# Spreading eight attention heads 3, 3, 2, 0 instead of 2, 2, 2, 2 over the four pairs of convolution chunks

## The chip, the cores and the metric

The kernel runs on one core of a Trainium2 chip. The metric is the device time of one execution in microseconds (us). Engines are named as in the profile: PE multiplies matrices (PEld loads its weights), DVE, ACT and POOL do elementwise work, SP issues nearly all DMAs. Each engine works through its own instructions strictly in the order in which they stand.

## The reference

One decoder layer for 512 tokens of width 2048, all in float32. Cut to what matters here:

```python
mod = silu(c) @ w_ada + b_ada                       # 6 sections of 2048 columns
shift1, scale1, gate1, shift2, scale2, gate2 = split(mod, 6)
h = rms_norm(x, norm1_g) * (1 + scale1) + shift1
cb, cc, ch, aq, ak, av = split(h @ w_in, ...)       # six blocks of 1024 columns
y_conv = cb * causal_conv3(cc * ch, conv_w)         # 1024 columns: 8 chunks of 128
for head in range(8):                               # two softmaxes per head
    p1, p2 = softmax(mask(q1 @ k1.T)), softmax(mask(q2 @ k2.T))   # 512 x 512 each
    y_attn[head] = rms_norm((p1 - lam * p2) @ v) * subln_g * (1 - lam_init)
x = x + gate1 * (concat(y_conv, y_attn) @ w_out)
h2 = rms_norm(x, norm2_g) * (1 + scale2) + shift2
# product-key expert layer: top-16 keys for 8 heads, 16384 single-neuron experts
x = x + gate2 * peer_ffn(h2, w_peer_q, sub_keys1, sub_keys2, expert_u, expert_v)
```

## The kernel before

Matrix products with weights are done in three passes: a number is split into a high part (by ACT, line 89) and the rest (by POOL or DVE, line 90), and PE adds high*high, high*rest and rest*high (`PASSES`). So every weight tile that lands (`wraw`, up to four in flight) passes ACT and then POOL before PE has all of it (`wsp`, three of them), and so does every activation tile.

The stages in the order of the code: norm and the first part of the modulation; the projections for q, k and v; then, around line 530, the stage that is changed; then the output projection (lines 545 to 607); then the expert layer, which takes most of the time.

**The changed stage** is a loop over four pairs of convolution chunks, `cp` = 0 to 3:

```python
nxt_head = 0
for cp in range(4):
    for _ in range(HEADS[cp]):
        head(nxt_head)
        nxt_head += 1
    if cp == 3:
        gw_ctx.close()
        ...
        xy = xy_ctx.enter_context(tc.tile_pool(name="xy", bufs=2, side="right"))
    conv(cp)
    if cp < 3:
        ada_later(ADA_N.pop(0))
```

- `head(h)` (lines 452 to 493) does one attention head in four blocks of 128 queries. In each block PE makes scores for both softmaxes (`sp`, line 461, and a mask, 463), DVE takes the maximum (464), ACT the exponential (466), DVE combines the two (469 to 471, `qk`), PE transposes (475), ACT copies (477, `aT`), PE multiplies with `vv` (480), ACT copies (482, `osb`) and sums squares. At the end of the head ACT takes a root (485), DVE scales (486, 489), PE transposes (490), ACT copies (492, `yt`), and a DMA stores the head (493, `y_dram`).
- `conv(cp)` (496 to 528) multiplies 256 columns of each of three blocks of `w_in` with the activations (507, 288 matrix products of 128x512 for a pair) and does the short convolution on DVE (518 to 527); two DMAs store `y_dram`. It also issues DMAs that lay expert rows out anew in DRAM (`lay_out`, line 249).
- `ada(...)` (192 to 222), called by `ada_later`, makes 512 columns of the modulation that is needed later: eight loads of 512 KB (`ada_w`, line 200, three buffers), sixteen multiply-adds on DVE (211, 215, `ada_acc`), four tiny PE products (219) and an addition (221). Three of these follow each of the first three pairs, nine in all. `ada_acc` and `ada_w` live in the pool `gw`.
- The output projection starts with loads of the sixteen chunks of `y` (552, `yr`, in the order `WO_ORDER`: chunks 0 to 5, 8 to 15, then 6 and 7) and of `x` (577, `xr`, four loads), both into the pool `xy`, which takes the place of `gw`: they can be issued only when the last `ada` is done with its memory. `yr` is split (`big`). There are four groups (`dg`) of 192 matrix products (593); group 0 needs all sixteen chunks, the others use them again. Each group ends with four additions on DVE (599). Between them twelve tiles of expert rows are loaded (561, `uar`, eight DMAs of 128 KB each, three buffers), transposed on DVE (570) and stored (571, 1 MB). PE also transposes `x` (581).

A scheduler orders the instructions when the program is built, by an estimate of its own of when each can run, with the order of the code as priority. So a head, which mostly waits for its own chain of engines, is not done before `conv` but woven into it and into what follows, on every engine.

Of the kernel before, what the change touches and what calls it, by code (L numbers as in the profile page):

```python
# [40 lines left out]
LAG = 3  # L41
PASSES = ((0, 0), (0, 1), (1, 0))
ADA_LATER = (0, 0, 0, 1, 2, 2, 2, 3, 3, 3)
HEADS = (2, 2, 2, 2)
WO_ORDER = (0, 1, 2, 3, 4, 5, 8, 9, 10, 11, 12, 13, 14, 15, 6, 7)
UR_BUFS = 2
BEGIN = 1
# [32 lines left out]
def hymba_peer(tc, x, c, positions, w_ada, b_ada, norm1_g, w_in, conv_w, q_norm_g, k_norm_g,  # L80
# [18 lines left out]
    with ExitStack() as ctx:  # L99
# [431 lines left out]
# [3 lines that stand above are left out]
# [580 lines left out]
```

## Time and profile before

| what | value |
|---|---|
| three runs of before: median (lowest, highest) | 3346.73 us (3344.19, 3349.19) |
| profiled execution, its own time | 3349.88 us |
| its span in the profile | 3347.6 us |
| PE busy | 3176.0 us, 95% of the span |
| DVE, ACT, POOL busy | 2739.1, 1223.3, 1057.7 us |
| moved by DMA | 1017.81 MB, 304 GB/s over the span |
| mean granted PE clock | 0.978 |

The time of an execution and its span differ by 2.3 us, which lie around the program. A busy share of the whole span is a mean over stages that have different limits, so the changed stage is read in windows of its own: it goes from about 384 us (first scores) to 733 us (last convolution product), and the output projection follows to 947 us.

### The profile page before, as it was taken

Reading aid. Unit: us, or ns where it says so; the run is one execution under the profiler, and the core shown is the slowest. Engines: PE = TensorE matmul, PEld = TensorE weight load, DVE = VectorE, ACT = ScalarE, POOL = GpSimd, SP = SyncE. Lnnn points to the kernel's source line nnn. Section 1 sums busy time; section 2 is a strip of 40 time slices with the busy share of each in tenths; the row PEclk is TensorE's granted clock in tenths of the full one; section 3 lists DMA queues with packets and bytes.
Section 4 is the critical chain, followed back from the end, with each engine's and each line's share of the span. In section 5 each row is a group of like instructions: output and inputs, shape, how many; then the busy total and the mean of one; then the engine's idle time right before and its main releaser. Section 6 shows DMA issues by size and latency. Waiting matters only on the chain.

```text
span 3347.6 us, 47029 instructions
## 1 busy us (share of the span) xinstructions
PE 3176.0 (95%) x18006; PEld 2945.2 (88%) x18006; DVE 2739.1 (82%) x3631; ACT 1223.3 (37%) x1866; POOL 1057.7 (32%) x709
## 2 busy tenths in 40 slices
PE   5889999999999859999999999999999999999998
PEld 4777877777777659999999999999999999999997
DVE  6888477842338998789999899999999999999975
ACT  5246343343255336632333333333333333333322
POOL 2447333353435634312222232222222222222210
PEclk9999999999999979999999999999999999999998
DMA  9878978966979878989989899998988898999964
GB/s 303 283 257 294 345 250 280 299 211 221 315 256 302 261 243 288 335 290 364 343 332 343 310 333 363 325 338 323 340 333 316 336 354 329 360 330 338 338 222 158
DMA packets 388896, 1017.81 MB, mean 304 GB/s; under 512 B 29713, under 2 KB 108478, under 8 KB 328126
## 3 DMA queue, kind: packets, MB, share of 16 engines
q1 hardware_dynamic: 342590, 679.23, 59.8%
q0 software_dynamic: 46080, 335.56, 25.7%
q8 instruction: 141, 2.31, 0.3%
q14 instruction: 85, 0.70, 0.1%
HBM read 965.11 MB, written 171.18 MB: 339 GB/s over the span
## 4 chain that ended last, share of the span: by engine, by line
PE 55%; DVE 4%; issue 2%; DMA 1%; ACT 0%; POOL 0%; DVEq 0%; ACTq 0%; SPq 0%; POOLq 0%
PE pa L835 26%; PE pv L1004 26%; PE pv L974 2%; DVE gacc L910 1%; DVE ut L90 1%; DMA xs<-x_dram 1%; DVE gt L963 1%; DVE ur L823 1%; DVE vs L90 1%; DMA gt<-in_expert_v_dram,idxu 0%; DMA gt<-in_expert_u_dram,idxu 0%; ACT ut L89 0%; DVE acc L1020 0%; PE pv L1061 0%; DVE gt L897 0%
## 5 line engine op out<-in xcount | busy, mean ns | idle before, releaser
L835 PE MATMUL pa<-hd,ut 128*128 128x352 f32 x6144 | 1067.2, 326 | 37.5 <-DVE ut L90 23.6
L1004 PE MATMUL pv<-W,vs 128*128 128x352 f32 x6144 | 1052.1, 325 | 5.1 <-ACT W L89 2.6
L835 PEld LDWEIGHTS pa<-hd,ut 128*128 128x128 f32 x6144 | 1010.9, 190 | 42.4 <-DVE ut L90 26.6
L1004 PEld LDWEIGHTS pv<-W,vs 128*128 128x128 f32 x6144 | 1001.8, 189 | 8.0 <-ACT W L89 3.5
L90 POOL TENSOR_TENSOR wsp<-wraw,wsp 128x1024 fp32r<-128x1024 f32 x160 | 389.0, 2434 | 557.6 <-ACT wsp L89 525.4
L89 ACT ACTIVATE vs<-vr 128x1024 fp32r<-128x1024 f32 x256 | 271.6, 1061 | 737.9 <-PE pv L1004 687.8
L89 ACT ACTIVATE ut<-ur 128x1024 fp32r<-128x1024 f32 x256 | 269.6, 1056 | 315.2 <-PE pa L835 239.5
L897 DVE SCALAR_TENSOR_TENSOR gt<-gt,h2n 128x2048 f32<-128x2048 f32 x160 | 364.6, 2283 | 18.3 <-DMA gt<-in_expert_u_dram,idxu 18.3
L910 DVE SCALAR_TENSOR_TENSOR gacc<-gt,ga_a,gacc 128x2048 f32<-128x2048 f32 x158 | 369.9, 2341 | 6.8 <-DMA gt<-in_expert_v_dram,idxu 6.7
L889 POOL DMA_INDIRECT gt<-in_expert_u_dram,idxu x128 | 183.0, 1430 | 554.6 <-DVE gt L897 320.8
L90 DVE TENSOR_TENSOR vs<-vr,vs 128x1024 fp32r<-128x1024 f32 x256 | 311.2, 1216 | 57.3 <-ACT vs L89 56.9
L90 DVE TENSOR_TENSOR ut<-ur,ut 128x1024 fp32r<-128x1024 f32 x256 | 310.9, 1219 | 55.6 <-ACT ut L89 54.4
L889 POOL DMA_INDIRECT gt<-in_expert_v_dram,idxu x128 | 172.4, 1347 | 552.3 <-DVE gacc L910 360.1
L89 ACT ACTIVATE wsp<-wraw 128x1024 fp32r<-128x1024 f32 x160 | 169.2, 1058 | 346.5 <-issue 72.0
L507 PE MATMUL pm<-big,wsp 128*128 128x512 f32 x1152 | 285.2, 401 | 0.0
L823 DVE STREAM_TRANSPOSE ur<-ur 128x1024 f32<-128x1024 f32 x232 | 274.5, 1221 | 0.1
L507 PEld LDWEIGHTS pm<-big,wsp 128*128 128x128 f32 x1152 | 214.9, 191 | 42.6
L282 PE MATMUL pqk<-wsp,big 128*128 128x512 f32 x768 | 190.1, 407 | 18.0 <-DVE qk L334 13.6
L748 PE MATMUL pm<-big,wsp 128*128 128x512 f32 x768 | 188.5, 403 | 19.0 <-POOL wsp L90 17.4
L282 PEld LDWEIGHTS pqk<-wsp,big 128*128 128x128 f32 x768 | 148.7, 196 | 53.0 <-DVE qk L334 17.0
L748 PEld LDWEIGHTS pm<-big,wsp 128*128 128x128 f32 x768 | 147.2, 195 | 52.2 <-POOL wsp L90 20.0
L593 PE MATMUL pm<-big,wsp 128*128 128x512 f32 x768 | 182.1, 397 | 6.2 <-DVE x L599 6.2
(274 smaller groups left out, 3024.0 us busy)
## 6 DMA issues: line engine op xcount, KB each, us to landing
ur<-u_dram SPq DMA_DIRECT2D x128, 1024.0 KB, 7.8
vr<-in_expert_v_dram SPq DMA_DIRECT2D x256, 512.0 KB, 7.2
u_dram<-in_expert_u_dram SPq DMA_DIRECT2D x464, 256.0 KB, 6.7
ada_w<-in_w_ada_dram SPq DMA_DIRECT2D x192, 512.0 KB, 5.5
wraw<-in_w_in_dram SPq DMA_DIRECT2D x96, 512.0 KB, 5.7
g_dram<-gtile SPq DMA_DIRECT2D x11, 2048.0 KB, 7.4
g<-g_dram SPq DMA_DIRECT2D x32, 704.0 KB, 9.4
wraw<-in_w_out_dram SPq DMA_DIRECT2D x32, 512.0 KB, 5.5
```

Source lines behind the costliest of these rows:

```text
L89: hi = nc.scalar.activation(dst[:, 0], src, AF.Copy)
L90: (eng or nc.vector).tensor_tensor(out=dst[:, 1], in0=src, in1=dst[:, 0].bitcast(F32), op=OP.subtract)
L282: nc.tensor.matmul(banks[i], hT[kk][:, a, i * P:(i + 1) * P], ws[:, b, k], start=(kk == last[0] and n == 0), stop=(kk == last[1] and n == 2))
L507: nc.tensor.matmul(banks[n2], ws[:, a, k, n2 * P:(n2 + 1) * P], hT[kk][:, b], start=(kk == 0 and n == 0), stop=(kk == KC - 1 and n == 2))
L593: nc.tensor.matmul(banks[j], ws[:, a, k, j * P:(j + 1) * P], yT[kk0 + k][:, b], start=(kq == 0 and k == 0 and n == 0), stop=(kq == 7 and k ...
L748: nc.tensor.matmul(banks[j], ws[:, a, k, j * P:(j + 1) * P], h2T[kk][:, b], start=(kk == 0 and n == 0), stop=(kk == KC - 1 and n == 2))
L823: nc.vector.transpose(t, t)
L835: mm = nc.tensor.matmul(pa[:, :TD], ut[:, a, j].rearrange("p b r -> p (b r)"), hd[k][:, b], start=(k == 0 and n == 0), stop=(k == KC - 1 a ...
L889: d = nc.gpsimd.indirect_dma_start(out=t, out_offset=None, in_=src, in_offset=bass.IndirectOffsetOnAxis(ap=gidx[g][:, j:j + 1], axis=0))
L897: return lambda: nc.vector.scalar_tensor_tensor(t, t, 1.0, h2n, op0=OP.mult, op1=OP.mult, accum_out=ga_a[:, j:j + 1])
L910: return lambda: nc.vector.scalar_tensor_tensor(gacc, t, a, gacc, op0=OP.mult, op1=OP.add)
L1004: mm = nc.tensor.matmul(pv[j // 2][:, j % 2, :TD], vs[:, a, bb, j * P:(j + 1) * P], W[e0 // 2][:, m, bb], start=(b == 0 and n == 0), stop= ...
```

## The change

```diff
-HEADS = (2, 2, 2, 2)
+HEADS = (3, 3, 2, 0)
```

In the code, heads 0 to 2 now stand ahead of pair 0, heads 3 to 5 ahead of pair 1, heads 6 and 7 ahead of pair 2, and none ahead of pair 3. The three groups of `ada` keep their places behind pairs 0, 1 and 2, so each of them now has more heads ahead of it in the order of the code. The instructions are the same in number and size. The scheduler weaves them otherwise on PE, DVE, ACT and SP, from the third head up to the end of the output projection; POOL keeps its order but for a few rows. Three places show it.

PE, where the convolution ends and the output projection begins (`pm<-big,wsp` is a matrix product; the number is that of the activation tile). Before:

```order
L507 MATMUL pm<-big_1457,wsp 128x512 x3
L475 MATMUL px<-ident,qk 128x128 x3
L507 MATMUL pm<-big_1467,wsp 128x512 x6
L507 MATMUL pm<-big_1477,wsp 128x512 x6
L593 MATMUL pm<-big_6025,wsp 128x512 x3
L461 MATMUL sp<-qk 128x128
L463 LDWEIGHTS identb
L463 MATMUL sp<-maskb,identb 128x128
L593 MATMUL pm<-big_6030,wsp 128x512 x3
```

Now, with seven rows between the last convolution product and these:

```order
L475 MATMUL px<-ident,qk 128x128 x3
L480 MATMUL px<-vv,aT 128x128 x3
L475 MATMUL px<-ident,qk 128x128 x4
L480 MATMUL px<-vv,aT 128x128 x4
L490 MATMUL px<-ident,osb 128x128
L219 MATMUL px<-ones,ada_acc 128x1 x4
L490 MATMUL px<-ident,osb 128x128 x3
L219 MATMUL px<-ones,ada_acc 128x1 x8
L593 MATMUL pm<-big_6025,wsp 128x512 x6
L593 MATMUL pm<-big_6030,wsp 128x512
```

Before, the first products of the output projection (593) follow those of the convolution at once, and the whole last head is woven into them. Now the tail of the last head and three tails of `ada` (219) stand between the two.

DVE, the last scaling of a head (486, 489) and what follows. Before, at the end of head 5, with the last `ada` behind it, head 6 under way and head 7 still to come:

```order
L486 RECIPROCAL os__4738<-os__4738 128x4
L489 TENSOR_SCALAR osb<-osb,os__4738 128x128 x4
L469 RECIPROCAL z<-z 128x2
L470 TENSOR_SCALAR z<-z,nlam 128x1
L471 SCALAR_TENSOR_TENSOR qk<-qk,z 128x256
L221 TENSOR_TENSOR modc<-px,vcol 128x4
L211 TENSOR_SCALAR ada_acc<-ada_w,scol 128x512
L215 SCALAR_TENSOR_TENSOR ada_acc<-ada_w,scol,ada_acc 128x512 x6
L221 TENSOR_TENSOR modc<-px,vcol 128x4
L215 SCALAR_TENSOR_TENSOR ada_acc<-ada_w,scol,ada_acc 128x512 x6
```

Now, at the end of the last head:

```order
L471 SCALAR_TENSOR_TENSOR qk<-qk,z 128x512
L486 RECIPROCAL os__4978<-os__4978 128x4
L489 TENSOR_SCALAR osb<-osb,os__4978 128x128 x4
L221 TENSOR_TENSOR modc<-px,vcol 128x4
L211 TENSOR_SCALAR ada_acc<-ada_w,scol 128x512
L215 SCALAR_TENSOR_TENSOR ada_acc<-ada_w,scol,ada_acc 128x512 x2
L221 TENSOR_TENSOR modc<-px,vcol 128x4
L215 SCALAR_TENSOR_TENSOR ada_acc<-ada_w,scol,ada_acc 128x512 x10
L570 STREAM_TRANSPOSE uar<-uar 128x512 x2
L215 SCALAR_TENSOR_TENSOR ada_acc<-ada_w,scol,ada_acc 128x512 x2
L570 STREAM_TRANSPOSE uar<-uar 128x512 x2
L215 SCALAR_TENSOR_TENSOR ada_acc<-ada_w,scol,ada_acc 128x512
```

The last `ada` (from 211) stood ahead of most of head 6, of all of head 7 and of the last steps of the convolution; now it stands behind all eight heads, with transposes of expert rows (570) among its steps.

SP, the first loads of the output projection. Before:

```order
L257 DMA wraw<-in_w_out_dram 128x2x512 x2
L249 DMA u_dram<-in_expert_u_dram 128x1x512 x4
L257 DMA wraw<-in_w_out_dram 128x2x512
L552 DMA yr<-y_dram 128x512 x3
L577 DMA xr<-in_x_dram 128x4x512 x2
L257 DMA wraw<-in_w_out_dram 128x2x512
L552 DMA yr<-y_dram 128x512 x3
L257 DMA wraw<-in_w_out_dram 128x2x512
```

Now:

```order
L200 DMA ada_w<-in_w_ada_dram 128x2x512
L561 DMA uar<-in_expert_u_dram 32x2x512 x14
L571 DMA u_dram<-uar 128x2048
L561 DMA uar<-in_expert_u_dram 32x2x512 x4
L552 DMA yr<-y_dram 128x512 x3
L577 DMA xr<-in_x_dram 128x4x512
L571 DMA u_dram<-uar 128x2048
L561 DMA uar<-in_expert_u_dram 32x2x512 x9
L577 DMA xr<-in_x_dram 128x4x512
L552 DMA yr<-y_dram 128x512 x3
L561 DMA uar<-in_expert_u_dram 32x2x512 x4
L571 DMA u_dram<-uar 128x2048
```

Before, the loads of `yr` came ahead of the first `uar`, the last three of them right ahead of it. Now 23 of the 96 `uar` loads and a store stand ahead of the first `yr`; from there to the last `yr` SP issues 57 loads of `uar`, 7 stores of it, the 4 `xr`, the 16 `yr` and 6 weight tiles.

## The prediction

> **What bounds the kernel now.** I read the page's header and busy shares first, then the chain of waits, then windows over the changed stage and the one behind it, then who waited for whom on PE in that stretch, and last the order of time of PE, DVE and SP around its end.
>
> ```profile
> span 3347.6 us, 47029 instructions
> ...
> PE 3176.0 (95%) x18006; PEld 2945.2 (88%) x18006; DVE 2739.1 (82%) x3631; ACT 1223.3 (37%) x1866; POOL 1057.7 (32%) x709
> ...
> PE 55%; DVE 4%; issue 2%; DMA 1%; ACT 0%; POOL 0%; DVEq 0%; ACTq 0%; SPq 0%; POOLq 0%
> ```
>
> PE is busy 95% of the span, and the shares by engine in the chain that ended last (third line) name hardly anything else. PE work can't be saved by a change that keeps every instruction, so only idle time of PE, or its clock, can move. Windows, with PE's busy time first and the DMA share and GB/s last:
>
> ```profile
> 384.00:733.00 349.00, 341.45 (x1565) 258.77 (x1563) 246.22 (x387) 137.76 (x303) 117.78 (x50) 0.98 0.81 270
> 733.00:949.00 216.00, 202.57 (x915) 162.88 (x913) 64.33 (x110) 75.08 (x121) 90.91 (x45) 0.98 0.78 246
> ...
> 733.00:784.00 51.00, 49.07 (x233) 37.40 (x231) 11.47 (x30) 27.15 (x59) 26.85 (x16) 1.00 0.36 115
> 811.00:911.00 100.00, 95.32 (x416) 78.52 (x416) 37.68 (x59) 25.46 (x30) 38.38 (x17) 0.97 1.00 313
> ```
>
> From the first scores to the last convolution product (384 to 733) PE idles 7.6 us of 349, in the output projection (733 to 949) 13.4 us of 216. That is all there is to gain: 21 us. The last two rows show how the cover works now. From 733 to 784 head 7 is woven into the output projection, PE stays busy, and the DMA engines are idle two thirds of the time. From 811 to 911 the DMA engines are full at 313 GB/s with the tiles of expert rows, and PE still works 95% of the time, because all sixteen `yr` are already there.
>
> Who made PE wait from 490 to 950 us (total, times, longest):
>
> ```profile
> PE pm L593 <- DVE x L599: 6.2, 2, 4.7
> PE px L581 <- DMA xr<-in_x_dram: 3.0, 1, 3.0
> PE sp L461 <- ACT qk L466: 2.2, 1, 2.2
> PE px L475 <- DVE qk L471: 2.2, 1, 2.2
> PE px L490 <- DVE osb L489: 2.0, 1, 2.0
> PE px L219 <- DVE cz L518: 1.5, 1, 1.5
> ```
>
> No wait is longer than 4.7 us. A head's chain costs PE 2 us here and there, because convolution or projection products stand between its steps.
>
> **The change, part by part.** *Heads moved forward.* Head 7 and the end of head 6 no longer lie in the output projection. PE's order puts ahead of the last convolution product two more score rows each of the three smaller sizes, nineteen more transposes and products, some masks, and twelve `ada` rows fewer. In the order of time of PE (start, us, count):
>
> ```profile
> 690.17 0.95 PE L219 MATMUL px<-ones,ada_acc 128*128 128x1 f32 x8
> 695.76 0.95 PE L219 MATMUL px<-ones,ada_acc 128*128 128x1 f32 x8
> ...
> 713.32 1.02 PE L219 MATMUL px<-ones,ada_acc 128*128 128x1 f32 x8 [1.49 <-DVE cz L518]
> ...
> 730.12 3.01 PE L507 MATMUL pm<-big,wsp 128*128 128x512 f32 x12
> ...
> 733.74 0.48 PE L461 MATMUL sp<-qk 64*128 64x128 f32 x2
> ...
> 736.50 0.60 PE L475 MATMUL px<-ident,qk 128*128 128x128 f32 x4
> ...
> 743.19 0.70 PE L461 MATMUL sp<-qk 64*128 64x256 f32 x2
> ...
> 749.85 0.91 PE L461 MATMUL sp<-qk 64*128 64x384 f32 x2
> ```
>
> Two rows each: 2 x (0.48 + 0.70 + 0.91) = 4.2; nineteen at 0.15 (0.60 for four) = 2.9; masks about 1; less three `ada` tails of 0.95: -2.9. Sum +5.2 us. The last convolution product, which ended at 730.12 + 3.01 = 733.1, now ends at 738. I leave the 7.6 us of idle time ahead of that as they are; the ends are 0 and, with each head's chain still there, twice that.
>
> *The tail of head 7 is bare.* Behind the last convolution product PE has only the end of head 7. On DVE and PE, its last block and its end before:
>
> ```profile
> 765.75 0.69 DVE L464 TENSOR_REDUCE z<-sp 128x1 f32<-128x512 f32 x1 [2.40 <-PE sp L463]
> ...
> 767.46 5.97 PE L593 MATMUL pm<-big,wsp 128*128 128x512 f32 x25
> ...
> 774.29 5.74 PE L593 MATMUL pm<-big,wsp 128*128 128x512 f32 x24
> ...
> 783.61 0.88 DVE L489 TENSOR_SCALAR osb<-osb,os__5493 128x128 f32<-128x128 f32 x4
> ```
>
> From the first maximum to the end of the scaling: 784.5 - 765.8 = 18.7 us, in which PE did 11.7 us of projection products between the head's own steps. Bare, the chain takes from 18.7 - 11.7 = 7 to 18.7; I take 11.5, nearer the lower end, since DVE and ACT still hand over to each other a dozen times, and 3 for the scores ahead of it. So DVE gets to the last `ada` at 738 + 14.5 = 752.5.
>
> *The last `ada` is bare too.* On DVE it now stands behind all of head 7, and on PE its products stand ahead of the first of the output projection, so PE waits for all of it. Before, it ran here, under convolution products:
>
> ```profile
> 691.24 0.62 DVE L211 TENSOR_SCALAR ada_acc<-ada_w,scol 128x512 f32<-128x512 f32 x1
> ...
> 710.30 2.87 DVE L215 SCALAR_TENSOR_TENSOR ada_acc<-ada_w,scol,ada_acc 128x512 f32<-128x512 f32 x1
> ...
> L215 DVE SCALAR_TENSOR_TENSOR ada_acc<-ada_w,scol,ada_acc x135: 730/752/2955, 407.6 to 710.3; 128x512 f32<-128x512 f32 x135
> ...
> L570 DVE STREAM_TRANSPOSE uar<-uar x48: 664/674/714, 799.6 to 908.7; 128x512 f32<-128x512 f32 x48
> ```
>
> That is 21.9 us, with a few convolution steps among it. By the median of 752 ns (third line; minimum, median, maximum) sixteen steps need 0.62 + 15 x 0.75 = 12 us. Now SP must also issue `uar` loads between the last `ada_w`, and four transposes of 0.67 us stand among the steps and wait for their loads. Ends 12 and 24; I take 21, near what it took then: the loads pace it, and they still do. It ends at 773.5.
>
> *The loads of `yr` come last.* Their pool takes over the memory of `ada_w`, so they can't be issued before that. PE's 0.95 us and four more `uar` issues go first: first `yr` at 775.5. Before, they were issued while convolution products still ran (start, time in the queue; below, a split of `yr` on ACT and on POOL in ns, and what the DMA engines moved in 40 slices of the span):
>
> ```profile
> 714.37 1.29 SPq L552 DMA_DIRECT2D yr<-y_dram  x3
> ...
> 788.40 2.69 SPq L552 DMA_DIRECT2D yr<-y_dram  x3
> 791.19 11.70 SPq L561 DMA_DIRECT2D uar<-in_expert_u_dram  x19
> ...
> 803.40 4.31 SPq L561 DMA_DIRECT2D uar<-in_expert_u_dram  x5
> ...
> 719.39 2.39 POOL L90 TENSOR_TENSOR wsp<-wraw,wsp 128x1024 fp32r<-128x1024 f32 x1 [6.77 <-DMA yr<-y_dram]
> ...
> L89 ACT ACTIVATE big<-yr x16: 615/632/644, 719.2 to 797.0; 128x512 fp32r<-128x512 f32 x16
> L90 POOL TENSOR_TENSOR big<-yr,big x16: 1282/1295/1610, 721.7 to 798.2; 128x512 fp32r<-128x512 f32 x16
> ...
> GB/s 303 283 257 294 345 250 280 299 211 221 315 256 302 261 243 288 335 290 364 343 332 343 310 333 363 325 338 323 340 333 316 336 354 329 360 330 338 338 222 158
> ```
>
> Issue to the first split took 5 us. So PE gets its first projection product at about 781, and from 738 to 781 it has some 10 us of work: **33 us of new idle time**.
>
> *The `uar` tiles stand ahead of `yr` in the queue.* From the first to the last `yr` SP issues 57 `uar` (128 KB), 7 stores (1 MB), 4 `xr` (1 MB), 16 `yr` (256 KB) and 6 weight tiles (512 KB): 7.5 + 7.3 + 4.2 + 4.2 + 3.1 = 26.3 MB. Group 0 needs every `yr`. At the 313 GB/s of the full window this takes 84 us, to 859.5; at the page's best slice, 364 GB/s, 72. PE's work in it is 192 products (43.8 us, the row at 806.83 below) and 64 `x` transposes (9.6 at 0.15), 53 us, so the transfers set the pace. The last pair is split (0.63 + 1.30) at 861.4.
>
> ```profile
> 806.83 43.82 PE L593 MATMUL pm<-big,wsp 128*128 128x512 f32 x192 [1.48 <-DVE x L599]
> ...
> 900.27 8.31 PE L593 MATMUL pm<-big,wsp 128*128 128x512 f32 x23 [4.68 <-DVE x L599]
> ...
> 908.78 38.59 PE L593 MATMUL pm<-big,wsp 128*128 128x512 f32 x169
> ```
>
> A product takes 38.59 / 169 = 0.228 us; but right behind the wait of 4.68 us twenty-three took 8.31, 0.361 each, 3 us lost: after an idle time PE runs slowly for some microseconds. The Trainium skill has this in "TensorE: Matmul & The Clock Gate", Part 1: after about 3.4 us idle the clock is halved, until about 3.4 us of work. The row agrees in kind, not in size: by the rule half of 3.4 us is lost, an estimate of 1.7, where the row has 3, and the sum would be 1.3 us lower.
>
> The last 24 products of group 0 take 5.5 + 3 us, to 869.9, and the additions 1.5 (the wait of 1.48 above): 871.4. Groups 1 to 3 took from 806.8 to 908.78 + 38.59 = 947.4, 140.6 us, with the 4.7 us wait, 3 us of slow products and sixteen `x` transposes (2.4 at 0.15), which all go: 130.5. **The projection ends at 1002 where it ended at 947: +55 us.** Behind it all engines have their old work, and PE bounds there, so nothing takes it back.
>
> Against the profiled execution (3349.88 us) that is 3405; its time is 3 us above the median of 3346.73, and against the median it is 3402.
>
> **The rivals.**
>
> *The queue keeps up (+25).* If `yr` slip through between the `uar` (8 `uar` in flight hide behind PE), group 0 takes its 53 us of work from 781, to 834; 1.5 for the additions, 130.5 for the rest and some 6 for waits end at 972, so +25: 3372. For it: 24 `uar` were issued in 17 us from 791 on (rows at 791.19 and 803.40), and 90 issues at that pace are 62 us, not 84. Against it: the row at 100% DMA share; from there on SP's order, not PE's need, decides.
>
> *Faster (-10).* The long waits of the output projection (4.7, 3.0, 2.0 and the 3 us of slow products) go, since heads and `uar` are out of its way, and the last `ada` is hidden. The point that decides: the bare stretch from the last convolution product to the first projection product must have under 13 us of idle time. With every lower end it has 3 + 7 + 12 + 5 = 27, less 10 of work = 17. It would give 3337 if the last `ada` found a place under the convolution, which DVE's order excludes.
>
> *The clock makes it worse (+73).* By rows: `yr` come in six batches now, and if PE waits for each and loses 3 us behind each, as in the row at 900.27, and none is hidden, that is 18 us more: 3420. Against it: a slow product while the next `yr` isn't there costs nothing. The Trainium skill's page on the clock gate, by its rule above, would make the six losses some 10 us, an estimate, and the time 3412.
>
> *No change (0).* If the order of issue mattered little because the same bytes and products remain, 3347. Against it: an engine can't pass a waiting instruction, and PE's first projection product stands behind the last `ada`.
>
> **How the numbers follow.** Chances: forecast 0.58, queue keeps up 0.22, clock 0.12, faster 0.05, no change 0.03. Faster or slower by 0.2% (7 us) is about what a measurement of this kernel can tell from no change. Slower: 0.92. The range reaches from just below the queue's case (3372) to the clock's (3420): 3366 to 3421, which leaves out the last two cases and part of the clock's, and takes in the ends of the tail (-4.5 to +7), the last `ada` (-9 to +3) and the rate (-12). The forecast's own range is 3385 to 3415.
>
> **What would show it.** In the profile after: one idle time of PE of 15 us or more ahead of a product of line 219 that DVE's `ada_acc` releases; the first projection product 40 us behind the last convolution product; PE's waits for `yr` splits (ACT or POOL `big`) of some 30 us in group 0 with a DMA share near 1.0; three last groups without a wait over 2 us and shorter than 133 us. Wrong would be: convolution products ending 20 us later or earlier than 738, or a first group of under 60 us.

## The result, and the profile after

The changed kernel takes 3390.57 us (median of 6 runs, 3383.50 to 3397.45) where the kernel before takes 3347.93 us on the same chip (6 runs, 3339.32 to 3350.70): a ratio of 1.0132, 95% interval 1.0113 to 1.0151, or +42.6 us. The profiled execution is the longest of the six: 3397.45 us, with a span of 3395.2 us. Against the profiled execution of before (3349.88 us) that is +47.6.

From the page of after, the header, the busy shares and the engines' shares in the chain that ended last:

```profile
span 3395.2 us, 47044 instructions
...
PE 3180.7 (94%) x18006; PEld 2949.6 (87%) x18006; DVE 2739.9 (81%) x3631; ACT 1223.9 (36%) x1866; POOL 1064.9 (31%) x709
...
PE 58%; DVE 1%; DMA 1%; issue 0%; ACT 0%; POOL 0%; SPq 0%; DVEq 0%; POOLq 0%; ACTq 0%
```

These lines barely show the loss, which is under 2% of the span. The windows show it. First before, then after, each cut at the last product of the output projection, near the last product of line 835 and at the end of PE's last product, some 4 us ahead of the end of the span (the columns: length, busy time of PE, PEld, DVE, ACT and POOL, the granted PE clock, the DMA share, GB/s):

```profile
384.00:947.00 563.00, 543.47 (x2476) 421.46 (x2473) 308.81 (x494) 210.85 (x422) 208.27 (x93) 0.98 0.80 261
947.00:3256.00 2309.00, 2235.83 (x13665) 2190.55 (x13664) 2104.71 (x2552) 823.05 (x1060) 669.85 (x508) 0.98 0.88 322
3256.00:3343.00 87.00, 74.03 (x422) 68.92 (x420) 47.56 (x117) 23.36 (x54) 0.00 (x0) 0.90 0.45 153
```

```profile
384.00:1004.00 620.00, 556.62 (x2487) 432.10 (x2485) 309.62 (x496) 211.29 (x422) 208.72 (x94) 0.93 0.74 239
1004.00:3310.00 2306.00, 2234.50 (x13676) 2190.72 (x13675) 2107.03 (x2553) 824.38 (x1061) 678.50 (x508) 0.99 0.89 322
3310.00:3391.00 81.00, 69.99 (x411) 64.97 (x409) 46.06 (x116) 22.34 (x53) 0.00 (x0) 0.92 0.47 162
...
735.00:786.00 51.00, 15.12 (x62) 11.72 (x61) 27.73 (x48) 9.99 (x25) 2.55 (x2) 0.55 0.72 215
786.00:873.00 87.00, 64.19 (x254) 51.07 (x255) 22.12 (x34) 25.40 (x39) 36.68 (x23) 0.81 1.03 319
873.00:1004.00 131.00, 131.00 (x579) 108.31 (x577) 26.97 (x33) 33.39 (x39) 57.56 (x24) 1.00 0.50 168
```

From 384 us to the end of the projection after is 57 us longer. PE idles 63.4 us there instead of 19.5 (+43.9), and is busy 13.1 us longer, at a clock of 0.93 instead of 0.98. Not all of the 57 us is the change: after comes to its first scores at 387.0 us, before at 384.6, although nothing is edited ahead of them (in the thirteen profiles of this document they start between 384.6 and 392.4). From the first scores to the end of the projection, with the same 2470 products in both, before and after are:

```profile
384.59:947.36 562.77, 543.24 (x2470) 421.04 (x2469) 309.17 (x494) 210.87 (x422) 208.27 (x93) 0.98 0.80 261
```

```profile
387.03:1004.31 617.28, 553.89 (x2470) 429.66 (x2469) 308.42 (x494) 211.27 (x422) 206.94 (x93) 0.93 0.74 239
```

That is +54.5 us: 43.9 of idle time and 10.6 in which the same products took longer. The last three rows of the table for after say where the idle time lies: 36 us of idle time between the two stages, 23 in group 0 while the DMA engines are full at 319 GB/s, none in groups 1 to 3. In the rest of the program after is 9 us shorter, 3 in the long stretch and 6 in the last. (Eleven products moved from the last stretch into the long one, 422 to 411, so the two parts aren't like for like; their sum is.)

PE in order of time around the join (start, duration, count, and in brackets the idle time ahead of the row and what ended it; the view ends at 872 us, so the last row shows only the first eight products of its run):

```profile
731.77 3.47 PE L507 MATMUL pm<-big,wsp 128*128 128x512 f32 x14
...
752.83 0.45 PE L490 MATMUL px<-ident,osb 128*128 128x128 f32 x1 [3.13 <-DVE osb L489]
...
755.31 1.71 PE L219 MATMUL px<-ones,ada_acc 128*128 128x1 f32 x8
777.09 1.84 PE L219 MATMUL px<-ones,ada_acc 128*128 128x1 f32 x8 [20.07 <-DVE ada_acc L215]
785.76 8.93 PE L593 MATMUL pm<-big,wsp 128*128 128x512 f32 x27 [6.84 <-ACT big L89]
...
815.83 1.94 PE L581 MATMUL px<-ident,xr 128*128 128x128 f32 x8 [5.05 <-DMA xr<-in_x_dram]
...
838.22 10.39 PE L593 MATMUL pm<-big,wsp 128*128 128x512 f32 x36 [7.53 <-ACT big L89]
...
868.63 3.78 PE L593 MATMUL pm<-big,wsp 128*128 128x512 f32 x8 [4.82 <-ACT big L89]
```

DVE's last `ada`, and SP's first and last load of `yr`:

```profile
754.89 0.48 DVE L211 TENSOR_SCALAR ada_acc<-ada_w,scol 128x512 f32<-128x512 f32 x1
...
766.74 1.54 DVE L215 SCALAR_TENSOR_TENSOR ada_acc<-ada_w,scol,ada_acc 128x512 f32<-128x512 f32 x2 [2.12 <-DMA ada_w<-in_w_ada_dram]
...
776.23 0.71 DVE L215 SCALAR_TENSOR_TENSOR ada_acc<-ada_w,scol,ada_acc 128x512 f32<-128x512 f32 x1
```

```profile
780.88 1.36 SPq L552 DMA_DIRECT2D yr<-y_dram  x3
...
861.24 0.37 SPq L552 DMA_DIRECT2D yr<-y_dram  x1
```

And who made PE wait from 480 to 1005 us (total, times, longest), where before no wait was over 4.7:

```profile
PE px L219 <- DVE ada_acc L215: 23.1, 3, 20.1
PE pm L593 <- ACT big L89: 21.5, 4, 7.5
PE px L581 <- DMA xr<-in_x_dram: 6.5, 2, 5.1
```

The two long waits are one coupling seen twice. PE stands for the last `ada`; `yr` may only be loaded once the memory of that `ada` is free; and by then the loads of expert rows stand between the `yr` in SP's queue.

### The profile page after: what moved, and what is told of

Same layout as the page of the kernel before. It is cut to its first block, busy times and chain, and to the rows that moved or that the text cites. A ratio compares the mean times of both kernels' runs of the same rounds, so it can differ in the third digit from the quotient of the medians.

```text
span 3395.2 us, 47044 instructions
## 1 busy us (share of the span) xinstructions
PE 3180.7 (94%) x18006; PEld 2949.6 (87%) x18006; DVE 2739.9 (81%) x3631; ACT 1223.9 (36%) x1866; POOL 1064.9 (31%) x709
## 4 chain that ended last, share of the span: by engine, by line
PE 58%; DVE 1%; DMA 1%; issue 0%; ACT 0%; POOL 0%; SPq 0%; DVEq 0%; POOLq 0%; ACTq 0%
PE pa L835 28%; PE pv L1004 28%; PE pv L974 2%; DMA xs<-x_dram 1%; DVE gt L963 1%; PE pv L1061 0%; DMA ur<-u_dram 0%; ACT vs L89 0%; DVE ur L823 0%; DVE vs L90 0%; DVE ut L90 0%; ACT ut L89 0%; DVE xs L1031 0%; POOL og L967 0%; DVE xs L1012 0%
## 5 line engine op out<-in xcount | busy, mean ns | idle before, releaser
L89 ACT ACTIVATE vs<-vr 128x1024 fp32r<-128x1024 f32 x256 | 271.7, 1061 | 734.7 <-PE pv L1004 679.8
```

Of the source, the lines that this page charges most:

```text
L89: hi = nc.scalar.activation(dst[:, 0], src, AF.Copy)
```

## The experiments

Each was run beside before (3343.86 us for the first two groups, 3343.89 for the third, 17 to 23 runs of it). The before of the result was 3347.93, 4 us more, so times of after and of an experiment are compared by what each loses against its own before. In the table, "conv" is where the last product of line 507 starts, "first" and "last" are the starts of the first and the last product of line 593, "rest" is the profiled execution's own time less "last". "Ahead" counts the heads that stand ahead of the last `ada` in the code.

| kernel | heads | ahead | conv | first | last | rest | median us (ratio to before) |
|---|---|---|---|---|---|---|---|
| before | 2,2,2,2 | 6 | 732.7 | 733.0 | 947.0 | 2402.9 | 1 |
| after | 3,3,2,0 | 8 | 734.8 | 785.8 | 1003.9 | 2393.6 | 3390.57 (1.0132) |
| e1_uar_behind | 3,3,2,0 | 8 | 737.5 | 778.5 | 975.5 | 2395.3 | 3366.61 (1.0067) |
| e2_y_own_memory | 3,3,2,0 | 8 | 744.3 | 744.5 | 950.9 | 2398.5 | 3345.58 (1.0005) |
| e3_ada_early | 3,3,2,0 | 6 | 724.5 | 757.9 | 974.6 | 2395.4 | 3371.30 (1.0087) |
| e4_heads_3212 | 3,2,1,2 | 6 | 717.6 | 728.6 | 949.5 | 2393.4 | 3342.31 (0.9995) |
| e5_heads_2330 | 2,3,3,0 | 8 | 734.5 | 784.6 | 1000.3 | 2393.2 | 3393.98 (1.0155) |
| e6_heads_2231 | 2,2,3,1 | 7 | 737.4 | 757.6 | 957.5 | 2395.6 | 3359.43 (1.0044) |
| e7_before_y_own_memory | 2,2,2,2 | 6 | 740.8 | 741.0 | 952.1 | 2401.0 | 3350.29 (1.0022) |
| e8_ada_342 | 3,3,2,0 | 8 | 724.9 | 775.9 | 985.4 | 2398.5 | 3385.00 (1.0119) |
| e9_own_1322 | 1,3,2,2 | 6 | 729.8 | 730.1 | 964.3 | 2393.4 | 3353.94 (1.0035) |
| e10_own_2312 | 2,3,1,2 | 6 | 724.3 | 724.6 | 959.5 | 2392.8 | 3356.45 (1.0043) |
| e11_own_3212 | 3,2,1,2 | 6 | 719.0 | 719.2 | 956.9 | 2399.3 | 3349.31 (1.0014) |

**What stands ahead of `yr` in the queue.** After, with every load of `uar` ordered behind the last `yr`:

```diff
-            nc.sync.dma_start(yr, y_dram[k])
+            yr_ld = nc.sync.dma_start(yr, y_dram[k])
...
-                    nc.sync.dma_start(t[s * 32:(s + 1) * 32, b:b + 2],
+                    tc.add_manual_dep(nc.sync.dma_start(t[s * 32:(s + 1) * 32, b:b + 2],
...
+                                      .rearrange("(b r) d -> r b d", r=32)).ins, yr_ld.ins.name, ORDER, reason="y first")
```

> Heads 3, 3, 2, 0 as in the changed kernel, and every load of expert rows (uar) is ordered behind the last load of y; nothing else is edited. Theory (the transfers ahead of y set the pace of group 0): the last ada still ends at about 773 to 777 us and the bare stretch stays, 30 to 35 us of idle time; but from the first to the last load of y it takes under 45 us instead of 80, group 0 is over at about 840 instead of 873, and the expert rows then load under groups 1 to 3 as in the kernel before. Projection ends at 980 to 985 instead of 1004; time about 3370, 18 to 24 us under the changed kernel. Rival (PE would wait as long for the splits of y, or for three y buffers, whatever is ahead in the queue): group 0 still takes 80 us, time within 5 us of the changed kernel (3391).

It takes 3366.61 us (5 runs, 3365.49 to 3370.80), ratio 1.0067 (1.0054 to 1.0080): it loses 22.8 us against its before, where after loses 42.6, so 20 us of the loss are gone. The projection takes 197 us from its first to its last product, after took 218. PE still waits for the last `ada`, but less. That `ada` takes 15.7 us on DVE instead of 22: DVE waits 3.4 us for its loads instead of 6.7, and no transposes of `uar` stand among its steps. So the idle time at the join is 26 us, less than the 30 to 35 expected, and the projection ends at 976, ahead of the 980 to 985 expected:

```profile
PE px L219 <- DVE ada_acc L215: 17.1, 3, 13.7
```

So about half of the loss comes from the `uar` ahead of and among the `yr`, most of it in the projection and the rest at the join, and the other half (+22.8 us against before) is the bare join.

**The memory.** After, with the pool `gw` kept until the projection is over, and `xr` in a pool of its own:

```diff
-                gw_ctx.close()
+                pass
...
-        xw = wo.enter_context(tc.tile_pool(name="xw", bufs=2))
+        xw = wo.enter_context(tc.tile_pool(name="xw", bufs=2)); xrp = wo.enter_context(tc.tile_pool(name="xrp", bufs=2))
...
-            xr = xy.tile([P, NT, 512], F32, name="xr")
+            xr = xrp.tile([P, NT, 512], F32, name="xr")
...
-        xy_ctx.close()
+        xy_ctx.close(); gw_ctx.close()
```

> Heads 3, 3, 2, 0 as in the changed kernel, but the loads of y get memory of their own: the pool of ada stays open until the projection is over, and the x tiles move to a pool on the other side. So y need not wait for the last ada; the order of heads and ada in the code is that of the changed kernel. Theory (the cost comes from y waiting for the memory of the last ada): projection products follow the convolution at once, no wait for ada_acc above 5 us ahead of them, projection ends at 945 to 957, time 3338 to 3352. Rival (the cost is in heads and ada being late on DVE and PE themselves, the memory only adds the last few us): the 20 us wait for ada_acc stays, and the time is 3370 or more.

It takes 3345.58 us (12 runs, 3339.07 to 3358.10), ratio 1.0005 (0.9994 to 1.0016): with the heads where after has them, the loss is gone. PE goes from the convolution into the projection, and head 7 is woven into it again (in the table PE's gap at the join, 51 us in after, is gone):

```profile
741.43 3.24 PE L507 MATMUL pm<-big,wsp 128*128 128x512 f32 x13
744.50 1.98 PE L593 MATMUL pm<-big,wsp 128*128 128x512 f32 x8
746.32 0.61 PE L480 MATMUL px<-vv,aT 128*128 128x128 f32 x4
```

The kernel before with the same edit tells whether the edit hides a cost:

> Heads 2, 2, 2, 2 with the edit of e2 (y and x loaded to memory of their own, that of the ada kept). Theory: yr are not late in before, so the edit has nothing to give: 3337 to 3350, within 0.2% of before. Rival (the edit gains 8 us or more by itself, and e2 only came out even because the order of the heads still costs that much): under 3336.

3350.29 us (12 runs, 3344.67 to 3360.90), ratio 1.0022 (1.0011 to 1.0033): just over the forecast, so the edit gives nothing by itself and rather costs some 6 us. Beside it, heads 3, 3, 2, 0 are no slower (3345.58). In these runs the order of the heads does harm only through that memory. The edit leaves two things joined: `yr` and `xr` no longer share a pool, and with the memory free the scheduler also orders PE otherwise, with products of the projection among the tails of `ada` again.

**How many heads stand ahead of the last `ada`.** `HEADS` alone, three ways:

```diff
-HEADS = (3, 3, 2, 0)
+HEADS = (3, 2, 1, 2)   # e4_heads_3212
+HEADS = (2, 3, 3, 0)   # e5_heads_2330
+HEADS = (2, 2, 3, 1)   # e6_heads_2231
```

> Heads 3, 2, 1, 2 with ada as before: two heads stand behind the last ada again. Built, the end of the projection stage is woven about as in the kernel before, but the last pieces of the whole program stand as in the changed kernel. Theory (the changed kernel gained 6 to 7 us at the end of the program by another weave of the final stores, and lost the rest at the convolution's end): projection ends at 943 to 953 and the stretch from the last product of line 835 to the end takes 80 to 82 us in the profile, not 87; time 3335 to 3345. Rival (those 7 us were chance): the stretch takes 86 to 88 and the time is 3343 to 3353.

> Heads 2, 3, 3, 0: two ahead of pair 0 as before, but again all eight ahead of the last three ada. Theory (what counts is how many heads stand ahead of the last ada): as with 3, 3, 2, 0, the last ada ends at 770 to 780, PE idles over 40 us between the last convolution product and the group's first full speed, the projection ends at 998 to 1008, time 3383 to 3398. Rival (the third head at the start of the stage does the harm): 3342 to 3365.

> Heads 2, 2, 3, 1: seven heads ahead of the last ada, where before had six and after has eight; in SP's order no uar stands ahead of a yr. Theory: only head 6 delays the last ada, PE waits for its end 5 to 20 us right behind the convolution, nothing is lost to the queue, 3350 to 3366. Rival one (a threshold at the eighth head): as before, 3337 to 3349. Rival two (any head more costs all of it): over 3380.

3342.31 us (12 runs, 3337.42 to 3350.34), ratio 0.9995 (0.9984 to 1.0005); 3393.98 (5 runs, 3392.05 to 3400.20), 1.0155 (1.0139 to 1.0171); 3359.43 (6 runs, 3352.78 to 3364.91), 1.0044 (1.0030 to 1.0059). All three times and ends of the projection came out as the theory said; only the idle time at the join of e5 was 33 us, not over 40. Six heads ahead cost nothing, even with three at the start; eight cost it all, even with two at the start; seven lie between. In e6 PE's wait at the join is there, but no `uar` stands between the `yr`:

```profile
734.68 3.11 PE L507 MATMUL pm<-big,wsp 128*128 128x512 f32 x13
737.63 0.95 PE L219 MATMUL px<-ones,ada_acc 128*128 128x1 f32 x8
752.21 1.84 PE L219 MATMUL px<-ones,ada_acc 128*128 128x1 f32 x8 [13.63 <-DVE ada_acc L215]
757.61 2.08 PE L593 MATMUL pm<-big,wsp 128*128 128x512 f32 x4 [1.66 <-ACT big L89]
```

**Moving the `ada` instead: two misses.** After, with four, five and no `ada` behind pairs 0, 1 and 2 (the last three numbers of the list), and with three, four and two:

```diff
-ADA_LATER = (0, 0, 0, 1, 2, 2, 2, 3, 3, 3)
+ADA_LATER = (0, 0, 0, 1, 2, 2, 2, 4, 5, 0)   # e3_ada_early
+ADA_LATER = (0, 0, 0, 1, 2, 2, 2, 3, 4, 2)   # e8_ada_342
```

> Heads 3, 3, 2, 0 as in the changed kernel, but the nine late ada stand behind pairs 0 and 1 (four and five) and none behind pair 2. Theory (what costs is the last ada behind all heads): its memory is free before the last heads, y is loaded ahead of the expert rows, projection ends at 945 to 957, time 3338 to 3352. Rival (heads moved forward cost by themselves, since the end of the convolution has nothing to weave): 3365 or more.

> Heads 3, 3, 2, 0 with three, four and two ada behind pairs 0, 1 and 2 instead of three each. In the order two tails of ada instead of three stand behind the last convolution product, no uar ahead of the first yr, 48 between the first and the last. Theory: the last ada ends some 10 to 20 us earlier than in after (756 to 766), yr begin right behind it, the queue still paces group 0 (24 MB, 75 us, to 835 to 848), projection ends 975 to 990, time 3362 to 3380. Rival (uar between the yr cost nothing, only those ahead of the first do): group 0 ends 53 us behind the first yr, time 3345 to 3359.

e3 takes 3371.30 us (5 runs, 3369.99 to 3378.96), ratio 1.0087 (1.0073 to 1.0102), where I expected no loss. The time lies in the rival's range, but e2 speaks against the rival: with the same heads it loses nothing. The PE rows of e3 show what it waits for:

```profile
689.92 0.95 PE L219 MATMUL px<-ones,ada_acc 128*128 128x1 f32 x8
...
695.50 0.95 PE L219 MATMUL px<-ones,ada_acc 128*128 128x1 f32 x8
...
714.42 1.50 PE L219 MATMUL px<-ones,ada_acc 128*128 128x1 f32 x8 [1.71 <-DVE ada_acc L215]
...
735.53 1.84 PE L219 MATMUL px<-ones,ada_acc 128*128 128x1 f32 x8 [10.61 <-DVE ada_acc L215]
752.37 1.84 PE L219 MATMUL px<-ones,ada_acc 128*128 128x1 f32 x8 [14.99 <-DVE ada_acc L215]
```

Earlier in the code was not early enough on the chip. Once bunched, the last three `ada` come 17 to 21 us apart, and two of them are left over when the convolution ends. From there to the last of them DVE is busy 19.8 of 27.4 us and waits 6.3 us for `ada_w`. The last ends at 752 us, 25 earlier than in after, but 39 later than in before, and `yr` comes after it, at 754.2.

e8 takes 3385.00 us (4 runs, 3379.52 to 3386.73), ratio 1.0119 (1.0101 to 1.0136), 5 us over my range. Two parts of it held: DVE ends the last `ada` at 759.4, and group 0 is paced by the queue (first to last `yr` 71 us), so the rival, by which `uar` between the `yr` cost nothing, falls. What failed is "`yr` begin right behind it": `yr` begin 13 us later. Two things hold them, and both wait for the end of the last head. In SP's order the store of that head (line 493) stands ahead of `yr`, and it is issued only when that head is done, at 771.7. On PE the last products of line 219, which read the memory of `ada`, stand behind the transposes of that head (line 490), and they end last, at 772.43:

```profile
770.72 1.71 PE L219 MATMUL px<-ones,ada_acc 128*128 128x1 f32 x8
```

```profile
771.68 0.34 SPq L493 DMA_DIRECT2D y_dram<-yt  x1
772.46 1.31 SPq L552 DMA_DIRECT2D yr<-y_dram  x3
```

So with the store out of the way `yr` would still have waited for PE.

More of heads 6 and 7 was left behind the convolution, which ended 10 us earlier than in after, and bare they took as long as the `ada` did: PE's gap from line 507 to line 593 is 51.0 us in both.

**What came back at the end of the program.** After and e4 have the same order on PE over its last 120 rows (equal products in a row taken as one), before and e2 another, and the time behind the projection goes with it. e4 was run for this too: from the last product of line 835 to the end of PE's last product it takes 79.4 us, just under the 80 to 82 expected, where after takes 81.0 and before 86.9. So its rival, by which those 6 us were chance (86 to 88), falls; but some 2 us of them are only the eleven products that stand ahead of the stretch in e4 as in after (an estimate, by the 1052.1 us of the 6144 products of line 1004). Three more kernels were to test this: the memory edit of e2, with heads that give these ends.

```diff
-HEADS = (3, 3, 2, 0)
+HEADS = (1, 3, 2, 2)   # e9_own_1322: the end of after
+HEADS = (2, 3, 1, 2)   # e10_own_2312: an end of its own
+HEADS = (3, 2, 1, 2)   # e11_own_3212: the end of before
```

> The edit of e2 (memory of their own for y and x) with heads 1, 3, 2, 2: six ahead of the last ada, and no wait between the last convolution product and the projection, since 30 projection products come ahead of the next tail of ada; at the end of the program PE has the order of after. Theory (the order at the end of the program makes the difference that came back): projection ends at 946 to 952, from there to the end of the execution 2393 to 2395 us in the profiled execution (after and the kernels with its end have 2393.2 to 2393.6, before 2402.9), time 3334 to 3344, below the two others of this group by 4 to 9. Rival (that part differs from run to run, not with the order): 2393 to 2403 without regard to the order, all three within 4 us of one another.

> As e9 with heads 2, 3, 1, 2: the same number of heads ahead of the last ada, but at the end of the program an order on PE that no kernel here had yet. Theory: projection ends at 946 to 952, the rest 2395 to 2401 us, time 3341 to 3350. Rival: as in e9.

> As e9 with heads 3, 2, 1, 2, the order of e4; at the end of the program PE has the order of before. Theory: projection ends at 946 to 952, the rest 2398 to 2403 us, time 3344 to 3352, slower than e9 by 4 to 9. Rival: as in e9.

3353.94 us (8 runs, 3348.98 to 3361.35), 3356.45 (6 runs, 3352.31 to 3360.82) and 3349.31 (12 runs, 3342.73 to 3356.25): ratios 1.0035 (1.0022 to 1.0048), 1.0043 (1.0030 to 1.0057) and 1.0014 (1.0004 to 1.0024). As a test by time it failed: the projections end at 957 to 964, not 946 to 952, and not alike, so e9 is not the fastest (e11 is, by 4.6 us). The rest of e10, 2392.8, also came out below the 2395 to 2401 expected. Head 7 now lies in group 0, where at its end no products are left to cover it, and in e11 PE waits up to 8.4 us for an `ada` that its own order puts behind the eleventh product of the projection. The column "rest" still tells something: with the end of after it is 2393.2 to 2393.6 in four kernels (after, e4, e5, e9), with that of before 2398.5 to 2402.9 in three (before, e2, e11). One wait goes with it, that of line 1061 for DVE's `xs`, over the last 80 to 87 us. Of before, then of after, e11 and e9:

```profile
PE pv L1061 <- DVE xs L1012: 5.0, 2, 3.0
```

```profile
PE pv L1061 <- DVE xs L1012: 1.6, 1, 1.6
```

```profile
PE pv L1061 <- DVE xs L1012: 4.6, 2, 2.8
```

```profile
PE pv L1061 <- DVE xs L1012: 1.5, 1, 1.5
```

That accounts for some 3 of the 9 us. The six kernels left out here, whose last rows on PE stand in other orders again, bear it out. In e10 the wait is 1.1 us and the rest 2392.8; in e1, e3, e6, e7 and e8 the wait is 4.6 to 5.0 us and the rest 2395.3 to 2401.0. So all thirteen profiles fall into two groups by this wait, and their rests don't overlap: five at 2393.2 on average, eight at 2398.3. By that some 5 of the 9 us go with the order that brings this wait. The other 4 are the spread among the eight, in which before has the longest rest. It stays a reading of one profile of each kernel, not shown by a time.

## Why the prediction was right, point by point

- *The whole*: 3402 us were forecast by the median, 3390.57 measured.
- *Heads moved forward*: the last convolution product was to end at 738 and ended at 735.2. Counted from the first scores it came no later than before (348.2 us behind them, before 348.5), so the +5.2 us did not come: PE was busy 2.5 us longer there and idle 2.9 us less, and the 2.1 us by the clock of the span are the later start.
- *The tail of head 7*: DVE was to reach the last `ada` at 752.5 and reached it at 754.9. From the last convolution product that is 19.7 us, where 14.5 were forecast, beyond the 11.5 chosen for the chain but within its upper end. That this term came out 5 us long and the one before it 5 short was luck. The products that had covered this chain were gone, and PE idled 1.4, 1.9, 1.4, 3.1 us and less between its steps.
- *The last `ada`*: 21 us were forecast; from 754.9 to 776.9 it took 22. Its loads paced it only in part: 12 us are its own steps on DVE, 6.7 are five waits for `ada_w` (the longest of 2.12 us), and 3.4 are transposes of `uar` among the steps and their wait.
- *First `yr` and first projection product*: 775.5 and 781 forecast, 780.9 and 785.8 measured. Idle time at the join: 33 forecast, 36 by the window.
- *The queue*: 84 us from the first to the last `yr` forecast, 80 measured (780.9 to 861.2), at 319 GB/s in the window of group 0. PE's waits for splits of `yr` in group 0 were to be some 30 us; without the 6.84 us ahead of its first product they are 14.6 for ACT's and 1.4 for POOL's, and 6.5 for `xr`. They are less because PE's own work took longer: its 180 products and 64 transposes ahead of the last wait were busy 60 us, not the 51 of full pace. e1 shows what the `uar` are worth: 20 us, less than the 30 by which forecast and first rival differ. Part of the 20 lies at the join, in the last `ada`, which I had not parted.
- *Groups 1 to 3*: 130.5 forecast, 131 measured without idle time. The projection ends at 1004.3; forecast 1002.
- *The step that failed* is the last one, "Behind it all engines have their old work, and PE bounds there, so nothing takes it back". Forecast +55, measured +57 at the end of the projection (+54.5 from the first scores), but +47.6 at the end of the execution: the scheduler had ordered the end of the program otherwise too, and 9 us came back there, some 5 of them with that order. The order of PE's last rows could be read before the run; I had compared it only up to the end of the output projection. The other 5 us between +47.6 and the medians' +42.6 are the spread of runs: the profiled after is 6.9 above its median, the profiled before 2.0.
- *The rivals*: the case that the queue keeps up needed group 0 done by 834; the last `yr` was issued at 861. The faster case needed under 13 us of idle time at the join; it had 36. No change is excluded by the interval (1.0113 to 1.0151). The clock's case (+73) held in its mechanism but not in its size. Behind the wait of 6.84 us, 27 products took 8.93 us instead of 6.2 (at 0.228), and behind 4.82 us the first eight took 3.78 instead of 1.8: 2.8 and 2.0 us, but most of the slow work ended while the next `yr` was still on its way.

The Trainium skill's "TensorE: Matmul & The Clock Gate", Part 1, says that the clock drops to half after an idle window of about 3.4 us and comes back after as much work. That the pace halves agrees: eight products of line 219 take 0.95 us ahead of e6's wait of 13.63 and 1.84 behind it. The length doesn't: the 2.8 us lost behind the wait of 6.84 us are, at half pace, 5.6 us of slow work, not 3.4.

## What to carry to other kernels

Before moving work in the code, look for what becomes free when that work ends: here a pool's memory, which only the first loads of the next stage needed, turned the 22 us of the last `ada` into a wait that PE could not fill and put those loads behind others in an in-order queue. Giving the loads memory of their own took the whole loss away, though it was no gain without the change. A forecast for a scheduled program must compare the orders to the end of the program, not to the end of the stage that was edited, since 9 of 57 us, some 5 of them with the new order there, came back 2300 us later.

## What I had not expected of the hardware

Slow products were more than I had counted: with the same products PE was busy 10.6 us longer, at a granted clock of 0.55 in the join and 0.81 in group 0. That is not 10.6 us of loss: in group 0 most of them ran while the next `yr` was still on its way. And the end of a bare head holds a step that I had left out: ACT loads a table for the root of line 485, 1.28 us, within the 6.47 us that DVE waits for it.

```profile
750.56 1.28 ACT L485 ACT_TABLE_LOAD   x1
```

```profile
752.18 0.18 DVE L486 RECIPROCAL os__4978<-os__4978 128x4 f32<-128x4 f32 x1 [6.47 <-ACT os__4978 L485]
```
